# Two DMA queues instead of one for the 6 MB tile loads of a running-maximum kernel

## The chip, the cores and the metric

The kernel runs on one core of a Trainium2 chip; the other cores do nothing. The metric is the device time of one execution in microseconds (us). "Before" is the kernel as it was, "after" the changed one.

Short names: SP, ACT, DVE, POOL and PE are the SyncE, ScalarE, VectorE, GpSimd and TensorE engines. SP and ACT each have a queue for DMA loads; 16 DMA engines do the transfers of both. A packet is one record of a DMA engine's work; for a tile it is one row of 48 KB. A dot is one of DVE's dot-product instructions.

## The reference

`x` is 8 x 2048 x 4096, `w` is 4096 x 1, both float32. 268 MB of `x` are read once.

```python
def reference(x, w):
    proj = (x @ w).squeeze(-1)
    cm = np.maximum.accumulate(proj, axis=1)
    is_record = (proj >= cm).astype(np.float32)
    return np.cumsum(is_record, axis=1).astype(np.float32)
```

## The kernel before

The first 1920 of the 2048 positions are handled as 40 tiles: five groups of 384 positions, eight batch rows each. A tile is 128 partitions x 48 KB (three positions of 16 KB per partition, 6.29 MB). Four tile buffers are used in turn. For each tile DVE makes the dot products of columns 0 to 2815, POOL multiplies the other 1280 columns by `w` and ACT adds them up. DVE and ACT each raise `fr` when they are done with a buffer, and the next load of that buffer waits for both. PE brings the sums of a group of eight tiles into place, and DVE then makes the two scans.

```python
        for k in range(NK):                       # NK = 40 tiles, NS = 4 buffers
            g, t = divmod(k, B)
            i = SY.dma_start(
                out=xbuf[k % NS],
                in_=x[B - 1 - t, g * N : (g + 1) * N, :].rearrange(
                    "(p r) d -> p (r d)", r=R
                ),
            ).then_inc(xs[k % NS], 16)
            if k >= NS:
                i._wait_ge(fr[k % NS], 2 * (k // NS))
            ...                                   # weights: one 16 KB load through ACT
            if t == NS and g:
                SY.dma_start(                     # 12 KB of output, 8 rows x 1.5 KB
                    out=out[:, (g - 1) * N : g * N], in_=cnt
                )._wait_ge(cs, g + 1).then_inc(od, 16)
...
            for t in range(B):                    # DVE, in a loop over the groups
                b, s = B - 1 - t, t % NS
                V.wait_ge(xs[s], 16).then_inc(go, 1)
                V.sem_inc(xs[s], -16)
                for j in range(R):
                    i = dot(...)
                i.then_inc(fr[s], 1)
```

The tail, the last 128 positions, comes as six loads of 2 MB ("rows" 0 to 5; 16 KB per partition) and nine smaller pieces, all through SP. They go into the buffers of tiles 36, 37 and 38, so each row load waits until one of these tiles is consumed. DVE does row 0, then the scans of the fifth group, then rows 1 to 5 and the pieces.

## Time and profile before

| | before |
|---|---|
| time, median of 2 runs | 631.58 us (631.44 to 631.71) |
| span of the profile | 630.1 us |
| DMA from 20 to 581 us | busy share 1.00, 433 GB/s |
| DVE, POOL, ACT busy | 64%, 59%, 28% |
| one tile load on the DMA engines | 14.50 us |
| DVE starts the last tile (39) at | 584.7 us |
| last load lands (packet and landing records) | 623.6 us |

The profile's first part (engine, busy us, share of the span, count) and its table of DMA queues (queue, packets, MB, share of the 16 engines' span). The DMA line between them is the busy share of the 16 DMA engines in tenths, in 40 equal slices of the span; q1 is SP's queue, q10 is ACT's:

```profile
PE 33.4 (5%) x100; PEld 14.7 (2%) x100; DVE 406.2 (64%) x295; ACT 177.7 (28%) x262; POOL 369.2 (59%) x137
...
DMA  9999999999999999999999999999999999999995
...
q1 hardware_dynamic: 8016, 268.50, 98.7%
...
q10 hardware_dynamic: 16, 0.02, 0.0%
```

The view of busy time by stretch, before: start and end, length, then the busy us (and count) of PE, its weight loads, DVE, ACT and POOL. The last three columns are TensorE's granted clock (a share of full speed), the DMA engines' busy share and their rate in GB/s:

```profile
20.00:581.00 561.00, 10.92 (x48) 5.92 (x48) 366.23 (x248) 159.44 (x234) 336.55 (x117) 1.00 1.00 433
581.00:600.00 19.00, 2.73 (x12) 1.47 (x12) 14.67 (x12) 6.53 (x9) 15.33 (x6) 1.00 0.99 426
600.00:621.00 21.00, 0.81 (x4) 0.38 (x4) 19.02 (x18) 6.98 (x12) 14.45 (x6) 1.00 1.00 422
```

The kernel is bound by the DMA engines from the first microseconds to the last load. The DMA issues (KB each, median us from issue to landing) show that SP is early, not late: a load needs 14.5 us of transfer and lands 47.8 us after its issue, so it has stood in line for more than two tiles.

```profile
xall<-in_x_dram SPq DMA_DIRECT2D x40, 6144.0 KB, 47.8
```

DVE's timeline at the end of the main loop, before (start us, duration, what; in brackets the idle time before it). The lines are the first dots of tiles 38 and 39, row 0, the first scan of the last group, and row 1:

```profile
570.13 3.09 DVE L120 CUSTOM_DVE_ANT_0 xall<-xall,w_v 128x2816 f32<-128x2816 f32 x1 [5.38 <-DVEq L238]
...
584.68 3.09 DVE L120 CUSTOM_DVE_ANT_0 xall<-xall,w_v 128x2816 f32<-128x2816 f32 x1 [5.44 <-DVEq L238]
...
593.71 3.08 DVE L120 CUSTOM_DVE_ANT_0 xall<-xall,w_v 128x2816 f32<-128x2816 f32 x1
...
597.38 1.00 DVE L135 TENSOR_TENSOR_SCAN cm<-ps,cm,small 8x384 f32<-8x384 f32 x1 [0.58 <-PE ps L273]
...
599.93 3.05 DVE L120 CUSTOM_DVE_ANT_0 xall<-xall,w_v 128x2816 f32<-128x2816 f32 x1
```

A tile costs DVE 9.0 us (584.68 to 593.71) and arrives every 14.5 us, so DVE waits 5.4 us for each: the wait on L238 is the wait for the tile's semaphore. Tile 38 is long done when 39 lands. The chain that ended last is the work followed back from the last instruction, at each step to what released it. Before (start us, us, what), it runs through the loads in the tail:

```profile
580.40 38.09 DMA xall<-in_x_dram
618.49 0.02 issue
618.51 1.62 DVE xall L120
```

### The profile page before, as it was taken

What the parts mean: (1) busy time and instruction counts of PE and PEld (TensorE: products, weight loads), DVE (VectorE), ACT (ScalarE), POOL (GpSimd) and SP (SyncE); (2) the same over time, 40 slices, a digit from 0 to 9 for tenths busy, and PEclk for the clock granted to TensorE, in tenths of its full rate; (3) what the DMA queues carried; (4) which work ended last, traced back from release to release, by engine and by line L of the source; (5) the groups of instructions that cost most, each with busy time, mean ns of one, the idle gap of its engine ahead of it and who ended that gap; (6) DMA issues with size and microseconds to landing.
All of it is one profiled execution on the core that took longest, in us unless ns stands there. A gap on an engine that the chain in (4) does not pass through costs nothing.

```text
span 630.1 us, 1239 instructions
## 1 busy us (share of the span) xinstructions
PE 33.4 (5%) x100; PEld 14.7 (2%) x100; DVE 406.2 (64%) x295; ACT 177.7 (28%) x262; POOL 369.2 (59%) x137
## 2 busy tenths in 40 slices
PE   8000000010000001000000010000001000000103
PEld 3000000000000000000000000000000000000001
DVE  0756666677655557766666675556667766555886
ACT  1322223233232222233232322222232322322332
POOL 0555666666555555666666555556666665555864
PEclk9999999999999999999999999999999999999999
DMA  9999999999999999999999999999999999999995
GB/s 385 415 446 443 412 443 444 422 434 440 424 437 441 431 427 443 440 415 446 438 421 440 440 424 437 440 425 434 440 440 418 443 440 418 444 437 417 425 431 209
DMA packets 8035, 268.55 MB, mean 426 GB/s; under 512 B 936, under 2 KB 1496, under 8 KB 2016
## 3 DMA queue, kind: packets, MB, share of 16 engines
q1 hardware_dynamic: 8016, 268.50, 98.7%
q8 instruction: 1, 0.02, 0.0%
q10 hardware_dynamic: 16, 0.02, 0.0%
q14 instruction: 2, 0.02, 0.0%
HBM read 268.45 MB, written 0.07 MB: 426 GB/s over the span
## 4 chain that ended last, share of the span: by engine, by line
POOL 52%; issue 38%; DMA 6%; PE 3%; DVE 0%; POOLq 0%; ACT 0%; SPq 0%; ACTq 0%
POOL xall L252 52%; DMA xall<-in_x_dram 6%; PE w_v L206 2%; PE ps L326 1%; PE ps L206 0%; DMA w<-in_w_dram 0%; DVE xall L120 0%; POOLq L255 0%; ACT w L216 0%; DVE cm_l L135 0%; DVE cnt_l L142 0%; SPq L176 0%; DVE rec_l L139 0%; ACT xall L126 0%; POOLq L247 0%
## 5 line engine op out<-in xcount | busy, mean ns | idle before, releaser
L120 DVE CUSTOM_DVE_ANT_0 xall<-xall,w_v 128x2816 f32<-128x2816 f32 (+3 forms) x135 | 389.3, 2931 | 185.8 <-DVEq L238 183.8
L252 POOL TENSOR_TENSOR xall<-xall,w_sb 128x1280 f32<-128x1280 f32 x120 | 345.2, 2903 | 246.0 <-POOLq L255 246.0
L126 ACT ACTIVATE xall<-xall 128x1280 f32<-128x1280 f32 x129 | 162.6, 1261 | 430.9 <-POOL xall L252 413.1
L273 PE MATMUL ps<-identity,small 128*8 128x128 f32 x60 | 13.6, 418 | 567.1 <-ACT xall L126 567.1
L294 POOL TENSOR_TENSOR xall<-xall,w_sb 128x1280 f32<-128x1280 f32 (+1 forms) x8 | 22.1, 2765 | 6.7 <-DMA xall<-in_x_dram 6.6
L126 ACT ACTIVATION_READ_ACCUMULATOR xall<-xall 128x1 f32 x129 | 24.0, 186 | 0.0
L273 PEld LDWEIGHTS ps<-identity,small 128*8 128x8 f32 x60 | 7.4, 130 | 574.4 <-ACT xall L126 570.6
L135 DVE TENSOR_TENSOR_SCAN cm<-ps,cm,small 8x384 f32<-8x384 f32 x6 | 6.0, 1004 | 15.0 <-PE ps L273 15.0
L206 PE MATMUL w_v<-w,identity 8*128 8x512 f32 x14 | 12.1, 1056 | 0.0
L224 DVE MEMSET ps<- 8x384 f32 x1 | 0.4, 378 | 17.1 <-ACT w L216 17.1
L120 DVE DVE_READ_ACCUMULATOR2_ANT small<- 128x1 f32 x135 | 11.0, 81 | 0.0
L326 PE MATMUL ps<-identity,small 128*1 128x128 f32 (+1 forms) x24 | 5.7, 407 | 22.9 <-DVE small L120 22.8
L142 DVE TENSOR_TENSOR_SCAN cnt<-rec,cnt,ps 8x384 f32<-8x384 f32 x6 | 6.0, 1002 | 0.2
L206 PEld LDWEIGHTS w_v<-w,identity 8*128 8x128 f32 x14 | 4.7, 333 | 7.3 <-issue 7.3
L213 ACT COPY w_sb<-w_v 128x768 f32<-128x768 f32 x1 | 0.8, 799 | 11.4 <-PE w_v L206 11.4
L139 DVE TENSOR_TENSOR rec<-ps,cm 8x384 f32<-8x384 f32 x6 | 3.3, 546 | 0.2
L326 PEld LDWEIGHTS ps<-identity,small 128*1 128x1 f32 (+1 forms) x24 | 2.1, 108 | 26.5 <-DVE small L120 25.0
L206 PE MATMUL ps<-w,identity 8*128 8x512 f32 x2 | 2.1, 1136 | 2.6 <-DMA w<-in_w_dram 2.6
L212 ACT ACT_TABLE_LOAD x1 | 1.3, 1283 | 1.6 <-SPq L148 1.6
L135 DVE TENSOR_TENSOR_SCAN cm_l<-ps,cm,small 8x128 f32<-8x128 f32 x1 | 0.5, 471 | 1.7 <-PE ps L326 1.7
L212 ACT COPY w_sb<-ps 128x512 f32<-128x512 f32 x1 | 0.6, 586 | 1.9 <-PE ps L206 1.9
L294 POOL TENSOR_TENSOR xall<-xall,w 128x320 f32<-128x320 f32 x1 | 0.9, 870 | 0.1
(15 smaller groups left out, 3.4 us busy)
## 6 DMA issues: line engine op xcount, KB each, us to landing
xall<-in_x_dram SPq DMA_DIRECT2D x40, 6144.0 KB, 47.8
xall<-in_x_dram SPq DMA_DIRECT2D x6, 2048.0 KB, 42.7
xall<-in_x_dram SPq DMA_DIRECT2D x1, 1344.0 KB, 36.7
xall<-in_x_dram SPq DMA_DIRECT2D x2, 384.0 KB, 30.5
xall<-in_x_dram SPq DMA_DIRECT2D x1, 704.0 KB, 38.1
xall<-in_x_dram SPq DMA_DIRECT2D x1, 640.0 KB, 39.1
xall<-in_x_dram SPq DMA_DIRECT2D x1, 224.0 KB, 21.7
xall<-in_x_dram SPq DMA_DIRECT2D x1, 192.0 KB, 21.8
```

Of the source, the lines that this page charges most:

```text
L120: return V.tensor_tensor_reduce(out=xsl, in0=xsl, in1=wsl, scale=1.0, scalar=0.0, op0=ALU.mult, op1=ALU.add, accum_out=dst,)
L126: return A.activation(out=xsl, in_=xsl, func=ACTF.Copy, accum_out=dst)
L135: V.tensor_tensor_scan(out=cm_, data0=ps[:B, :n], data1=neg.to_broadcast([B, n]), initial=cm0, op0=ALU.max, op1=ALU.max,)._wait_ge(psr, ba ...
L139: V.tensor_tensor(out=rec_, in0=ps[:B, :n], in1=cm_, op=ALU.is_ge)._wait_ge(psr, base + 1).then_inc(psr, 1)
L142: V.tensor_tensor_scan(out=cnt_, data0=rec_, data1=zero.to_broadcast([B, n]), initial=cnt0, op0=ALU.add, op1=ALU.add,)._wait_ge(psr, base ...
L206: i = T.matmul(out=dst, lhsT=identity[:NW, k : k + 1].to_broadcast([NW, P]), rhs=w_row, start=True, stop=True,).then_inc(bw, 1)
L212: A.copy(out=w_sb[:, CV - VC :], in_=ps)._wait_ge(bw, 1).then_inc(wc, 1)
L213: A.copy(out=w_sb[:, : CV - VC], in_=w_v[:, VC:CV])._wait_ge(bw, NW).then_inc(wc, 1)
L252: i = G.tensor_mul(out=xl, in0=xl, in1=w_sb).then_inc(pl, 1)
L273: i = T.matmul(out=ps[:B, j:N:R], lhsT=l[:, j * B : (j + 1) * B], rhs=identity, start=k == 0, stop=k == 1,)
L294: G.tensor_mul(out=xl, in0=xl, in1=w_pool(*p))._wait_ge(landed, 16).then_inc(pl, 1)
L326: i = T.matmul(out=ps[:m, :P], lhsT=l[:, :m], rhs=identity, start=k == 0, stop=k == len(parts) - 1,)
```

## The change

The intent is to take half of the loads off SP and give them to ACT's queue, so that two queues feed the DMA engines. Tiles 0, 2, 4, ... stay on SP. Tiles 1 and 3 are issued by ACT at the start, the other odd ones from inside ACT's own work, right after ACT's part of the tile that frees the buffer; for that, ACT's loop over the groups is unrolled. The tail stays on SP.

```diff
-        for k in range(NK):
+        def tile_load(k, q):
             g, t = divmod(k, B)
-            i = SY.dma_start(
+            i = q.dma_start(
                 out=xbuf[k % NS],
 ...
             if k >= NS:
                 i._wait_ge(fr[k % NS], 2 * (k // NS))
+
+        for k in range(NK):
+            g, t = divmod(k, B)
+            if k % 2 == 0:
+                tile_load(k, SY)
+            elif k < NS:
+                tile_load(k, A)
 ...
-        with A.Fori(0, NG):
+        for g in range(NG):
             for t in range(B):
 ...
                 i.then_inc(fr[s], 1)
                 A.sem_inc(pl, -R)
+                k = g * B + t + NS
+                if k % 2 and k < NK:
+                    tile_load(k, A)
```

## The prediction

> **What bounds the kernel now.** The 16 DMA engines: from 20 to 581 us their busy share is 1.00 at 433 GB/s (busy time by stretch), and the SP queue fills 98.7% of the span (queue table). In the packet records nearly every 48 KB packet takes 1.815 us on its engine, eight per engine and tile: one 6.29 MB tile per 14.50 us. All 268.5 MB at that rate take about 620 us; the rest is 2 us before the first packet and 7 us after the last load. DVE (64%) and POOL (59%) wait for each tile; in the timeline DVE idles 5.4 us before most. SP is not short of time: an issue takes 0.33 us, a load 47.8 us from issue to landing, 3.3 tiles of queue. No issue comes late.
>
> **What the change does.** 20 of the 40 tile loads move to ACT's queue, 0.33 us of issue each on an engine 28% busy. Bytes, packet sizes, buffers and arithmetic stay. SP's saving is off the critical path. The Trainium skill ("DMA: Bandwidth & Descriptors", "Issuing engines are not separate DMA queues") says SP's and ACT's DMAs run on the same 16 engines and interleave; the trace shows these saturated, so I expect no rate gain.
>
> The order changes. The same page ("Queues, rings and completion order") says each engine takes turns between queues, packet by packet. The packet records agree: an 8 KB instruction packet (309 ns) ran between two 48 KB packets in mid-tile. So the tiles of a pair (SP's even, ACT's odd) should share the engines: 29 us of transfer each, landing about 1.8 us (one packet) apart instead of 14.5.
>
> In the main loop that is free: a pair needs 2 x 9.1 us of DVE (plus 6 at a group's end), under 29. ACT's buffer is free about 20 us after landing, so each queue has its next tile 10 us ahead; the last load ends where it did (about 622 us).
>
> At the end it is not free. Before, tile 38 is computed while 39 loads; DVE starts 39 at 584.7 us. After, 38 lands about 583 and 39 about 584: a backlog of one tile. Estimate from traced durations, on DVE: start 583; tiles 38 and 39, 2 x 9.03 -> 601; row 0 -> 604; PE and scans -> 607; five rows x 3.01 -> 622; nine pieces 6.9 -> 629; then 5.9 us from last dot to end, as before -> 635 (637 if 38 lands no sooner than 39). The span was 630.1: +5 to +7 us, all on the critical path. The tail turns from load-bound to DVE-bound.
>
> **Prediction.** 637.2 us, 8 in 10 between 631.3 and 640.5. Faster by over 2%: 0.01; within 2%: 0.93; slower by over 2%: 0.06.
>
> **What would show it.** (1) Queue table: two queues, about 126 and 142 MB; 433 GB/s in the middle. (2) DVE works on two tiles back to back (18 us), then idles about 11. (3) From 585 to 622 us DVE has hardly any idle time; before, it waits 1.5 us for a row there. (4) The chain that ended last goes through DVE dots, not POOL and DMA; the last load still lands near 622.
>
> **What would make it wrong.** If engines take a whole load before changing queue, the order stays: 631.6. If changing queue costs time per packet (after two instruction packets the next 48 KB packet took 0.25 and 0.53 us longer), it is slower by several per cent; I think the next packet is fetched ahead. If the pair drifts apart by half a tile, the backlog shrinks.

## The result

| | before | after |
|---|---|---|
| time, median of 2 runs | 631.58 us | 637.57 us (637.50 to 637.63) |
| ratio, 95% interval | | 1.0094 (1.0075 to 1.0114) |
| span of the profile | 630.1 us | 635.8 us |
| DMA from 20 to 581 us | 1.00, 433 GB/s | 1.00, 434 GB/s |
| DVE starts tile 38 / tile 39 | 570.1 / 584.7 us | 585.0 / 594.1 us |
| last load lands | 623.6 us | 624.6 us |
| last dot of DVE ends | 624.2 us | 630.7 us |

A ratio is the mean time of one kernel's fast runs over the mean of the other's fast runs of the same rounds, so it is not quite the ratio of the medians. The interval says that after is slower by about 0.9%.

The queues, after. Half of the tile bytes now come through q10:

```profile
PE 32.1 (5%) x100; PEld 14.8 (2%) x100; DVE 404.5 (64%) x295; ACT 177.6 (28%) x262; POOL 368.3 (58%) x137
...
DMA  9999999999999999999999999999999999999991
...
q1 hardware_dynamic: 5136, 142.67, 52.1%
q10 hardware_dynamic: 2896, 125.85, 45.7%
```

Busy time by stretch, after:

```profile
20.00:581.00 561.00, 10.91 (x48) 5.88 (x48) 357.21 (x243) 155.38 (x228) 327.29 (x114) 0.72 1.00 434
581.00:600.00 19.00, 0.00 (x0) 0.00 (x0) 14.97 (x9) 6.17 (x9) 15.11 (x6) 0.50 0.98 421
600.00:621.00 21.00, 2.73 (x12) 1.48 (x12) 20.78 (x18) 10.19 (x16) 21.00 (x8) 0.58 1.00 422
```

The main loop moves the same bytes at the same rate. What differs is how far DVE has come with them: up to 581 us DVE had done 9.0 us less work (366.23 less 357.21), which is one tile. From 600 to 621 us DVE is busy for 20.78 of 21 us and POOL for all 21. DVE's timeline, after, for the same five instructions as before:

```profile
585.03 3.09 DVE L120 CUSTOM_DVE_ANT_0 xall<-xall,w_v 128x2816 f32<-128x2816 f32 x1 [7.31 <-DVEq L245]
...
594.06 3.08 DVE L120 CUSTOM_DVE_ANT_0 xall<-xall,w_v 128x2816 f32<-128x2816 f32 x1
...
603.09 3.08 DVE L120 CUSTOM_DVE_ANT_0 xall<-xall,w_v 128x2816 f32<-128x2816 f32 x1
...
606.33 1.00 DVE L135 TENSOR_TENSOR_SCAN cm<-ps,cm,small 8x384 f32<-8x384 f32 x1 [0.15 <-PE ps L283]
...
608.88 3.05 DVE L120 CUSTOM_DVE_ANT_0 xall<-xall,w_v 128x2816 f32<-128x2816 f32 x1
```

Tile 39 has landed by 584.7 us, as before (584.4), but DVE starts it at 594.06, because tile 38 landed at the same time. From there DVE runs to its last dot without a wait for a load. The chain that ended last, after, shows it: where before had one stretch of 38 us of DMA, it now has one dot after the other from 608.95 us on (some of the lines). Before that, from 587.75 to 602.12 us, it goes through POOL's products of tiles 38 and 39; for what came of them DVE's scan waited only 0.15 us.

```profile
608.95 2.98 DVE xall L120
...
611.94 3.00 DVE xall L120
...
614.95 3.00 DVE xall L120
...
617.96 3.00 DVE xall L120
```

The granted TensorE clock in the profile is 0.72 after and 1.00 before. It plays no part here: in the rounds of the first experiments, runs of before with a clock of 0.622 took 631.95 and 632.06 us, and those with 0.998 to 1.0 took 630.81 to 632.39.

### The profile page after: what moved, and what is told of

Read it like the earlier page. It is cut to its first block, busy times and chain, and to the rows that moved or that the text cites. A ratio compares the mean times of both kernels' runs of the same rounds, so it can differ in the third digit from the quotient of the medians.

```text
span 635.8 us, 1228 instructions
## 1 busy us (share of the span) xinstructions
PE 32.1 (5%) x100; PEld 14.8 (2%) x100; DVE 404.5 (64%) x295; ACT 177.6 (28%) x262; POOL 368.3 (58%) x137
## 3 DMA queue, kind: packets, MB, share of 16 engines
q1 hardware_dynamic: 5136, 142.67, 52.1%
q10 hardware_dynamic: 2896, 125.85, 45.7%
## 4 chain that ended last, share of the span: by engine, by line
POOL 48%; issue 44%; DVE 3%; PE 3%; DMA 0%; POOLq 0%; ACT 0%; ACTq 0%; SPq 0%
POOL xall L259 48%; DVE xall L120 3%; PE w_v L213 2%; PE ps L336 1%; DMA w<-in_w_dram 0%; PE ps L283 0%; PE ps L213 0%; DVE cm L135 0%; DVE cnt L142 0%; ACT w L223 0%; DVE rec L139 0%; POOLq L262 0%; DVE cm_l L135 0%; DVE cnt_l L142 0%; POOLq L254 0%
```

## The experiments

Twelve kernels were run. "Landing" below is read from the records of each tile's semaphore: each of the 16 DMA engines raises it once, so a tile has a first and a last landing, and the spread is the difference. DVE can start at the last. Each run but one was timed in 3 rounds against before on the same chip; medians of before were 631.42 to 632.15 us there.

**The theory.** Each DMA engine takes packets from the two queues in turn. The two tiles of a pair then land together. In the main loop that only moves DVE's idle time; at the end it leaves a backlog of one tile (9 us) on DVE, of which before's waits in the tail absorb a part. **Rival A**: mixing two queues costs the engines time all along the loop (the mean rate over the span fell from 426 to 422 GB/s). **Rival B**: the later start (the first dot begins at 31.6 us instead of 21.1). **Rival C**: the lower clock, or the unrolled loop.

### The last pair in order, the other 19 pairs mixed

```diff
-            if k % 2 == 0:
+            if k % 2 == 0 or k >= NK - 2:
                 tile_load(k, SY)
 ...
-                if k % 2 and k < NK:
+                if k % 2 and k < NK - 2:
```

> The change, but tiles 38 and 39 both go through SP, in order; tiles 0 to 37 alternate as in the change. Theory (backlog of one tile at the end, because the last pair lands together): 38 lands about 14.5 us before 39, DVE finds no backlog, the tail is load-bound again: 631.6 us (631 to 632.5), although 38 of 40 tiles are mixed as before. Rival A (mixing two queues costs the DMA engines time along the whole loop): 19 of 20 pairs are still mixed, so about 637. Rival B (the late start: first dot at 31.6 us instead of 21.1): start unchanged, so 637.6. Rival C (the lower granted TensorE clock of the changed kernel's profile): 637 if the clock is near 0.72 here too.

Measured: 632.37 us, ratio to before 1.0009 (0.9992 to 1.0026), correct. The clock in the profile was 0.715 and the first tiles landed as late as in after. Tile 38 landed at 570.1 us and 39 at 584.6. The timeline of DVE in this run has tile 39 start where it does before, after an idle wait:

```profile
573.86 3.08 DVE L120 CUSTOM_DVE_ANT_0 xall<-xall,w_v 128x2816 f32<-128x2816 f32 x1
...
584.88 3.09 DVE L120 CUSTOM_DVE_ANT_0 xall<-xall,w_v 128x2816 f32<-128x2816 f32 x1 [1.91 <-DVEq L245]
```

So the loss is not spread over the loop (A), does not come from the start (B), and not from the clock (C).

### Only tile 39 through ACT

```diff
+            if k < NK - 1:
                 tile_load(k, SY)
 ...
-                if k % 2 and k < NK:
+                if k == NK - 1:
                     tile_load(k, A)
```

> Only tile 39 goes through ACT, all else through SP. Tile 39 is issued when tile 35 is consumed, then shares the engines with SP's tiles 36 and 37 and lands before 38; tile 38 lands last, about 584 us, and DVE has 38 and 39 still to do then. Theory: one mixed tile at the end costs as much as the whole change or a little more, 637 to 639 us. Rivals A and B (cost along the loop, late start): 631.6 to 632, as 39 of 40 tiles go as in the kernel before.

Measured: 637.39 us, ratio 1.0096 (1.0079 to 1.0114), correct. Tile 39 landed at 569.4 us, ahead of 38 at 584.5. DVE takes tiles in order, so it sat idle for 18 us while 39 took its share of the engines and 37 was late, and when 38 had landed it had 38 and 39 to do. The lines are the first dots of tiles 37, 38 and 39:

```profile
570.25 3.09 DVE L120 CUSTOM_DVE_ANT_0 xall<-xall,w_v 128x2816 f32<-128x2816 f32 x1 [18.15 <-DVEq L243]
...
584.75 3.09 DVE L120 CUSTOM_DVE_ANT_0 xall<-xall,w_v 128x2816 f32<-128x2816 f32 x1 [5.38 <-DVEq L243]
...
593.78 3.08 DVE L120 CUSTOM_DVE_ANT_0 xall<-xall,w_v 128x2816 f32<-128x2816 f32 x1
```

One load in the other queue costs as much as twenty. Together with the run above this settles where the time went.

### The unrolled loop alone

```diff
-            if k % 2 == 0:
-                tile_load(k, SY)
-            elif k < NS:
-                tile_load(k, A)
+            tile_load(k, SY)
 ...
-                if k % 2 and k < NK:
+                if False:
```

> Control: ACT's loop is unrolled as in the change, but all loads go through SP. Theory: 631.6 us (within 0.1%). If the unrolling (instruction fetches, ACT's program) had part in the loss, it is over 632.5.

Measured: 632.09 us, ratio 1.0006 (0.9989 to 1.0023), correct. Unrolling has no measurable cost.

### All tiles through ACT, the tail through SP

```diff
-            if k % 2 == 0:
-                tile_load(k, SY)
-            elif k < NS:
+            if k < NS:
                 tile_load(k, A)
 ...
-                if k % 2 and k < NK:
+                if k < NK:
```

> All 40 tiles go through ACT, the tail rows through SP as ever. In the main loop one queue alone has work, so order and rate are those of the kernel before. At the end SP's rows are free to start when tile 36 is consumed and then share the engines half and half with tiles 37, 38 and 39. Theory (equal turns between queues): 39 lands about 615 us instead of 584, after most rows, and the kernel takes about 660 us (655 to 665). If queues were served in order of issue, 631.6.

Measured: 640.17 us (one run, state unknown), correct. Slower, as the theory has it, but by 8 us and not by 28. Tile 38 landed at 576.3 us together with row 0 (574.6), and tile 39 at 595.6 together with row 1 (593.9). DVE's timeline in this run, first dots of tiles 38 and 39:

```profile
576.57 3.09 DVE L120 CUSTOM_DVE_ANT_0 xall<-xall,w_v 128x2816 f32<-128x2816 f32 x1 [10.94 <-DVEq L243]
...
595.88 3.09 DVE L120 CUSTOM_DVE_ANT_0 xall<-xall,w_v 128x2816 f32<-128x2816 f32 x1 [10.20 <-DVEq L243]
```

That corrects one detail of the theory: the turns are by packet, not by bytes. A tile has eight packets of 48 KB on each engine, a row eight packets of 16 KB. One tile and one row take 8 x 1.815 us + 8 x 0.611 us, 19.4 us together (the times of a 48 KB and of a 16 KB packet in the records), and 576.3 to 595.6 is 19.3 us. The expectation had halved the bytes. This run was timed once; a run that shows the same follows below (`e10`).

### The pair apart by a quarter, a half and a whole tile: three misses

If the time depends on how far apart the last two tiles land, then ACT's queue can be made to start later, and the time should follow. The first two edits let ACT's first load wait for the first or the third of the small weight matmuls; the third puts ACT's first two loads behind its three weight copies.

```diff
             if k >= NS:
                 i._wait_ge(fr[k % NS], 2 * (k // NS))
+            elif k == 1:
+                i._wait_ge(bw, 1)          # half: 3
```

```diff
-            elif k < NS:                   # whole
-                tile_load(k, A)
 ...
         A.copy(out=w2, in_=w_v[:, W2 : W2 + WC]).then_inc(wc, 1)
+        for k in (1, 3):
+            tile_load(k, A)
```

> The change, but ACT's first tile load waits for the first weight matmul, so that ACT's queue starts about 3 us after SP's (a quarter of a tile's time). Theory (backlog at the end depends on how far apart the tiles of the last pair land): ACT's tiles land about 7 us after SP's instead of 2; 39 lands a few us later than in the change and DVE waits less for 38: worked out with equal sharing about 633 us (632 to 635.5). Rival A (cost of mixing along the loop): 637.6, as all pairs are mixed.

> As the run before, with ACT's queue starting half a tile's time (about 7 us) after SP's. Theory: tiles land evenly, 14.5 us apart, but tile 39 lands about 7 us later than in the kernel before, behind a share of the first rows: worked out about 635 us (633.5 to 637). In the main loop the landings are even, about 14.5 us apart, as in the kernel before. Rival A: 637.6.

> ACT's first tile loads are placed behind its three weight copies, so that ACT's queue starts when SP's first tile has landed (about 18.5 us). Theory: the pairs that land together are 1 with 2, 3 with 4, and tile 39 shares with the tail rows: it lands about 598 us instead of 584, DVE idles before it and then has all rows to do: worked out about 643 us (641 to 646). The last load still lands near 623 us. Rival A: 637.6 or less, as less is mixed at the start.

Measured: 638.05, 638.20 and 638.10 us, ratios 1.0095, 1.0098 and 1.0093, all correct. All three expectations failed: the offset made no difference. The traces say why: it did not last. These are landings, first to last engine in us, read from the semaphore records:

```text
                tile 0        tile 1        tile 12        tile 13        tile 36        tile 38        tile 39
after            30.1- 31.3    33.7- 34.9   204.2-205.3    206.0-208.9    552.3-559.3    581.3-584.8    576.8-584.7
quarter offset   26.6- 29.4    35.7- 37.7   200.6-203.4    206.4-211.7    548.8-557.5    577.8-584.7    578.4-585.3
half offset      22.8- 24.3    40.9- 42.4   196.9-198.4    211.4-216.3    545.0-555.8    573.9-584.7    579.6-587.4
whole offset     17.4- 18.3    48.3- 49.2   192.8-194.2    215.2-219.5    541.3-553.8    570.4-584.8    583.3-588.0
```

Up to tile 12 the offset holds and the engines stay about as close as at the start: 1.6 us apart at most in after and the half offset, 2.9 us in the quarter offset (from its first tile on) and for one tile, 11, of the whole offset. At tile 13 they come apart further, and at the end they differ by 7, 11 and 14 us for tile 38 in the three offset runs. Its slowest engine lands at 584.7 or 584.8 us in all four, and DVE waits for the slowest. So DVE started tile 39 at 594.0 to 594.1 us in all of these runs, as in after. The theory of the backlog stands with that (same start of tile 39, same time), but what pulled the engines apart was open.

### What pulls the engines apart: the output stores

The first output store (12 KB, eight rows of 1.5 KB, so eight packets on part of the engines) stands in SP's queue right behind tile 12. The packet records carry queue, size and time, but not the engine; engines were told apart by the rule that a packet starts when another one ends. Two of the engines in after, about 190 to 214 us, put together in this way (S and A: a 48 KB packet of SP and of ACT; s and a: the 4-byte semaphore packet that ends a load or store; o: a 1.5 KB packet of the store):

```text
without a store packet:   A S A S A S A s A S a S A S A
with a store packet:      S A S A S A S A s A o a s A S A S A
```

The turns alternate strictly, whatever the size of the packet; eight of the 16 engines carry a store packet. On the second engine the store spent two of SP's turns (o and its s), and ACT got ahead. Call this theory W. Its test is to leave the four stores of the main loop out. That gives a wrong result (1536 of the 2048 output columns stay unwritten), with the semaphore raised by hand:

```diff
-                SY.dma_start(
-                    out=out[:, (g - 1) * N : g * N], in_=cnt
-                )._wait_ge(cs, g + 1).then_inc(od, 16)
+                SY.wait_ge(cs, g + 1)
+                SY.sem_inc(od, 16)
```

This edit was put on after, on the half offset and on the whole offset.

> The change without the four 12 KB output stores of the main loop (their outputs stay unwritten: wrong on purpose; the semaphore is raised by hand). Theory W: each engine gives each queue one packet in turn, whatever its size, so a 1.5 KB store packet spends one of SP's turns, and ACT gains 48 KB on the eight engines that carry the store; that is what pulls the 16 engines apart (spread of a tile's landings 1.2 us early, 7 us late in the changed kernel). Without the stores the spread stays under 2 us to the end, SP's tile of each pair lands 3 to 4 us before ACT's to the end, DVE starts tile 38 near 583.3 and 39 near 592.4 instead of 594.1: about 636 us (635 to 637). If something else (waits at a group's end, instruction fetches) pulls them apart, landings and time stay as in the change: 637.6 to 638.1.

> The half-tile offset of the earlier run, now without the four stores (wrong on purpose). Theory W with the backlog theory: the offset now lasts, spread under 2 us, tile 38 lands near 576 and tile 39, which shares with the rows packet by packet (48 KB against 16 KB), near 586 to 588; DVE starts 39 near 587 to 589 instead of 594: about 632 us (631.4 to 634), although all pairs are mixed. If the offset is lost by another cause: 638.

> The full offset (ACT's first loads behind the weight copies), now without the four stores (wrong on purpose). Theory W: tiles 37 and 38 land together near 570, 39 shares with the first three rows at three bytes to one and lands near 589.5; DVE starts 39 near 590: about 633.5 us (632 to 635). If queues shared by bytes, 39 would land near 597 and the time be about 641; if the offset is lost anyway, 638.

Measured, in this order: 635.56 us (ratio 1.0043, 1.0002 to 1.0085), 631.81 us (0.9985, 0.9944 to 1.0026) and 633.04 us (1.0003, 0.9962 to 1.0044). The intervals are wide because one run of before in these rounds took 636.33 us; the kernels' own four runs each agree within 1.2 us. All three times fell where theory W put them. Without stores the spread of tile 36 is 1.2 us in the first of them (7.0 in after) and 2.9 us in the second (10.8 with stores). One detail of the second expectation failed: the spread was to stay under 2 us, but it was 3.1 us at tile 0 already and stayed at about 3 us. The first is 2 us faster than after (637.57 us, in other rounds). The two intervals of the ratio just overlap, so for these 2 us the traces are the better evidence: DVE starts tile 39 at 591.7 us instead of 594.1. In the third, tile 39 landed at 589.4 us; the expectation had 589.5 for sharing by packets and 597 for sharing by bytes. In the run with the half offset and no stores, the timeline of DVE has tile 38 start at 577 and tile 39 at 588 us, and DVE waits for both, although every pair is mixed:

```profile
577.16 3.09 DVE L120 CUSTOM_DVE_ANT_0 xall<-xall,w_v 128x2816 f32<-128x2816 f32 x1 [3.28 <-DVEq L246]
...
587.76 3.09 DVE L120 CUSTOM_DVE_ANT_0 xall<-xall,w_v 128x2816 f32<-128x2816 f32 x1 [1.49 <-DVEq L246]
```

Leaving out the stores might have saved time by itself. Two more runs close that way. The first leaves them out of the kernel with all loads on SP (wrong again).

> Control for the runs without stores: all loads through SP (ACT's loop unrolled), the four stores left out (wrong on purpose). If the stores cost nothing by themselves, the time is that of the kernel before: 631.6 to 632.1. If leaving them out saved time by itself (the other reading of the runs without stores: 638 to 632 for the half offset), it is 626 to 630.

Measured: 631.37 us, ratio 0.9995 (0.9979 to 1.0012). The stores cost nothing measurable by themselves.

The second makes all stores, but half of each through either queue, so that both queues lose the same turns; the counts of the store's semaphore are doubled to match.

```diff
                 SY.dma_start(
-                    out=out[:, (g - 1) * N : g * N], in_=cnt
+                    out=out[:, (g - 1) * N : g * N - N // 2], in_=cnt[:, : N // 2]
                 )._wait_ge(cs, g + 1).then_inc(od, 16)
 ...
+                if t == 0 and g:               # ACT, after its part of the group's first tile
+                    A.dma_start(
+                        out=out[:, g * N - N // 2 : g * N], in_=cnt[:, N // 2 :]
+                    )._wait_ge(cs, g + 1).then_inc(od, 16)
```

> A right version of the half offset: all four stores are made, but each in two halves by columns, one through SP and one through ACT, so that both queues spend the same number of turns on the same eight engines. Theory W: the offset lasts as without stores, tile 39 lands near 587.5 and DVE starts it near 588: 631.5 to 633.5, and the result is correct. If what pulls the queues apart is the writing itself and not the turn it takes, the offset is lost: 638.

Measured: 632.48 us, ratio 1.0016 (0.9999 to 1.0033), correct. DVE starts tile 38 at 576.1 and tile 39 at 588.2 us. The spread of tile 38 is 1.8 us (10.7 in the half offset with all stores on SP). What mattered about the stores was the turn, not the writing.

### All profiled runs in one table

Times are us from the start of the span; "39 to end" is the end of the span less DVE's start of tile 39.

| run | 38 landed | 39 landed | DVE starts 39 | end of span | 39 to end |
|---|---|---|---|---|---|
| before | 569.9 | 584.4 | 584.7 | 630.1 | 45.5 |
| last pair in order (`e1`) | 570.1 | 584.6 | 584.9 | 631.0 | 46.1 |
| unrolled, all SP (`e3`) | 570.1 | 584.6 | 584.8 | 629.8 | 44.9 |
| all SP, no stores (`e11`) | 569.7 | 584.2 | 584.5 | 629.7 | 45.3 |
| half offset, no stores (`e9`) | 576.9 | 587.5 | 587.8 | 630.1 | 42.3 |
| half offset, stores split (`e12`) | 575.8 | 587.9 | 588.2 | 630.4 | 42.2 |
| whole offset, no stores (`e10`) | 571.4 | 589.4 | 589.7 | 632.0 | 42.3 |
| after, no stores (`e8`) | 582.4 | 584.9 | 591.7 | 633.8 | 42.1 |
| only 39 through ACT (`e2`) | 584.5 | 569.4 | 593.8 | 635.3 | 41.6 |
| after | 584.8 | 584.7 | 594.1 | 635.8 | 41.8 |
| quarter offset (`e4`) | 584.7 | 585.3 | 594.0 | 636.7 | 42.6 |
| half offset (`e5`) | 584.7 | 587.4 | 594.0 | 636.6 | 42.6 |
| whole offset (`e6`) | 584.8 | 588.0 | 594.1 | 636.7 | 42.6 |
| all ACT (`e7`) | 576.3 | 595.6 | 595.9 | 638.4 | 42.5 |

The span ends about 42 us after DVE starts tile 39, or at about 630 us when the last loads set the end (the first rows of the table). Start of tile 39 explains every run within about 1 us. No version beats the kernel before: the best mixed ones reach it, and in every run the last load lands between 623.5 and 624.7 us.

## Why the prediction was right

The predicted time was 637.2 us, the measured one 637.57. Point by point:

1. *The DMA engines bound the kernel, no issue comes late, moving issues gains nothing.* Right: 433 GB/s before, 434 after, busy share 1.00 in both. The Trainium skill ("DMA: Bandwidth & Descriptors", "Issuing engines are not separate DMA queues") says that loads of different issuing engines run on the same 16 DMA engines; this trace agrees (after, the packets of q1 and q10 take 52.1% and 45.7% of the span of the same 16 engines).
2. *Each engine takes turns packet by packet, so pairs land together.* Right, shown by the packet order and by the landings: 31.3 and 34.9 us for tiles 0 and 1, where before had 18.9 and 33.4. The size of the gap was off: 3.6 us (31.3 to 34.9) and not one packet of 1.8; the semaphore packet that ends a load takes a turn too, as the order of packets shows. A cost of changing the queue, which the prediction named as a risk, does not show: the median 48 KB packet takes 1.815 us in both kernels.
3. *The main loop pays nothing.* Right: DVE works two tiles back to back and then idles 10.9 us (11 predicted), and the run with only the last pair set in order is as fast as before.
4. *The tail turns from load-bound to DVE-bound by a backlog of one tile.* Right, and shown by the two runs that undo and that isolate the last pair. DVE's milestones were predicted as 601, 604, 607, 622, 629 and measured as 603.1, 606.1, 608.9, 623.9, 630.7. The chain that ended last goes through DVE's dots only from 608.95 us on; the prediction's "not POOL" does not hold for the 14 us of tiles 38 and 39 before it.
5. *Tile 38 lands about 583 us.* This was off by 2 us: DVE started it at 585.0. The prediction had the other case as an aside ("637 if 38 lands no sooner than 39") without a reason for it. The reason is the output stores' turns: without them DVE started 38 at 582.7 and the time was 635.56.
6. *5.9 us from the last dot to the end, as before.* It was 5.1 us (630.7 to 635.8): before, the small matmuls had a queue behind the last dot (the last scan waited 1.7 us for PE), after only 0.9 us. Why the wait differs is not shown: in the half offset, where DVE starts tile 39 at the same time as in after, it is 1.8 us again, which is also why that run ends 0.8 us later. Points 5 and 6 partly cancel, so the closeness of 637.2 to 637.57 is better than the sum deserves.
7. *The last load still lands near 622 us.* It was 624.6 by the landing records; before has 623.6 by the same records, so 622 was read too roughly, and after is 1.0 us later. The record shows part of this 1 us: at 610.0 us an 8 KB instruction packet (309 ns) ran on one engine, the next 16 KB packet there took 0.851 us instead of 0.611, and from then on a row's landings spread over 2.3 us instead of 1.7. The runs without such a packet after tile 36 (before, `e2`, `e3`, `e11`) have their last landing at 623.5 to 623.8 us, those with one at 624.1 to 624.7. No run tested this. It costs nothing here, as DVE ends 6 us later.
8. *If the pair drifts apart by half a tile, the backlog shrinks.* True for a pair held apart on all engines (631.81 and 632.48 us), but the drift that really happened was between engines, and it kept the backlog (638.20 us).

## What to carry to other kernels

When loads already queue up in front of full DMA engines, as here (433 and 434 GB/s), a second queue brings no bytes sooner; it only changes which load finishes first, and the last loads are where that shows, because the work behind them can no longer hide. Ask of every stream of loads in what order they land on the slowest engine and how much work is still undone when the last one lands; if two queues are needed for other reasons, put the last few loads back on one queue in the order in which they are consumed. Here the queues shared by packets: a 1.5 KB store packet in one of them spent the same turn as a 48 KB one and shifted everything behind it.

## What the Trainium skill lacked or had wrong

- "DMA: Bandwidth & Descriptors", "Queues, rings and completion order", says that engines take turns between queues at packet granularity and gives about 9 to 17 descriptors as a typical packet. The turns are confirmed. For these loads, though, the turn changed after every single 48 KB row (one record of 1.815 us), not after several. That a row is a single descriptor is not shown by a run.
- The same section does not say what follows for unequal packets: shares go by packets, not by bytes. With 48 KB packets in one queue and 16 KB packets in the other, a 6.29 MB tile and a 2.1 MB row landed together (576.3 and 574.6 us, then 595.6 and 593.9, in the run that was timed once).
- No page says that a load's 4-byte semaphore packet and a store's 1.5 KB packet spend a whole turn. Four 12 KB stores in one of two busy queues pulled the 16 engines 7 us apart (tile 36; 1.2 us without them) and cost 2 us of time (637.57 against 635.56 us, in different rounds; spans 635.8 and 633.8).
- "Rules for kernel authors" on the same page says that spreading loads over the issuing engines does not help bandwidth and only saves issue time. The rate agrees (433 and 434 GB/s), but it is not neutral: the changed landing order cost 5.7 us of span (630.1 to 635.8). No page says what the changed order can cost.
